# A gated recurrence's level products repacked to 128x128, with the second half of the tokens reversed

## The chip, the cores and the metric

One core of a Trainium2 chip runs the whole kernel in one launch. The metric is the device time of one execution in microseconds (us). TensorE is called PE, its weight loads PEld, VectorE DVE, ScalarE ACT, GpSimd POOL, and SyncE SP, which here only issues loads of weights and inputs.

## The reference

Two decoder layers over 256 tokens of width 1024, in float32, each followed by a SwiGLU feed-forward block (FFN). Layer 0 mixes tokens with a gated linear recurrence (8 heads, 128 key features each), layer 1 with causal attention and a relative-position bias. The change is mostly in layer 0:

```python
q = silu(q); f = lb + (1 - lb) * sigmoid(fz); k = 1 - f
S_t = diag(f_t) S_{t-1} + k_t i_t^T          # per head
o_t = S_t^T q_t
```

Written as scores this is `score[t, s] = sum_n q[t,n] k[s,n] prod(f[s+1..t, n])` for s <= t, and `o = score @ i`. The diagonal `score[t, t] = sum_n q[t,n] k[t,n]` has no decay. In layer 1, with 256 tokens in one block, attention is plain causal attention: `softmax(q k^T / sqrt(128) + bias[t - s])`.

## The kernel before

**Products.** A float32 matrix product is made of three products of the type fp32r: every operand is split into a rounded high part and a remainder (`whi`, `wlo` of a weight, `xh`, `xl` of an activation), and PE adds high x high, high x low, low x high (`mm_w`, L479, moves 256 tokens per product; `mm_x`, L488, moves 512 weight columns). These are called weight products here. Weights come from memory in pieces of 128x1024 (`raw`, issued on SP, L401); ACT rounds each (L412) and DVE takes the remainder (L414), six pieces ahead. The products of the recurrence itself are plain f32, issued by `mm` (L454).

**A head of the recurrence** (`class Core`, L724). Features lie on partitions, tokens on columns. Three projections of 24 weight products each come one after another, forget, query and gate, and their work goes on while PE makes the next ones.
- `forget` (L736): sigmoid, `f` and `k1 = 1 - f` on ACT; six products on POOL (`tot`, L752) give the decay over 2, 4, ... 64 tokens.
- `query` (L755): silu into `mov` on DVE, `q1 = q f`, and ACT puts the odd columns of `q1` behind `mov`.
- `step` (L778), for m = 1, 2, ... 32: from the queries and keys of blocks of m tokens to those of 2m: DVE scales the later half of the queries (L785) and the earlier half of the keys (L787) by the decay of the other half, ACT copies the other halves over (L789, L792). So a block's queries are scaled by the decay since its start, and its keys by the decay until its end. At m = 32 ACT makes two rearranging copies more (L799, L801), and for 64 `last` (L809) scales the queries and keys that meet across token 128.
- `scores` (L816): PE multiplies keys by queries. The scores within a pair of blocks of m tokens are one "level"; a mask picks the right entries. The diagonal and level 1 come from two products of 192 columns (128 from `mov`, 64 from `q1`), levels 2, 4, 8, 16 from two products of 64 columns each (one for either half of 128 tokens), levels 32 and 64 from two products of 128 columns (`both`, L857), and the tokens across 128 from one (L862). DVE's `copy_predicated` (L844, L827) moves each level from PSUM into the score tile `pm` under its mask; ACT moves the large blocks (`far`, L866, five copies). `values` (L880) multiplies `i` by `pm`, 256 and 128 columns. Token order is ascending, so in either half of 128 tokens the later tokens look back at the earlier ones.

**The order of the work.** `Order` (L136) simulates the engines with nominal costs while the program is built. An instruction goes to its engine's queue when the simulated clock finds its inputs ready, the lowest due time first; instructions of PE outside the weight products are put in only when their inputs have been ready for 1500 ns by those costs (`early`, `pick` L218). The queues of the engines are in that order on the chip, and each waits for its inputs on semaphores.

**Bias and final factors.** A table of the bias by distance (384 distances) is made by one product (L937) and written to memory, and eight loads issued by POOL (L941) spread it into `bt`, 128x(8x256). The final norm's gains are later loaded into the same place (`gf`, L1136, issued on ACT) and scaled on ACT (L1137).

**Names that the prediction uses.** psA and psB are the two sets of four PSUM banks. `pv` holds the norm gains, loaded by a DMA that ACT's queue issues (L517). `sqacc` and `ny` are the row statistics of a norm.

Of the kernel before, what the change touches and what calls it, by code (L numbers as in the profile page):

```python
# [8 lines left out]
FT = mybir.dt.float32  # L9
# [6 lines left out]
P = 128  # L16
# [13 lines left out]
LEVELS = (1, 2, 4, 8, 16)  # L30
# [252 lines left out]
def cv(n, fast=False):  # L283
    return ((n / 2 if fast else n) + 66) / 0.96
# [18 lines left out]
def hybrid_trunk(ctx: ExitStack, tc: tile.TileContext, wts, xT, par, gfin, tab, onehot, masks, out):  # L303
# [14 lines left out]

    def new(tag, shape, bufs=1, dt=FT, held=False):
        return ring(tag, shape, bufs, dt).new(held)  # L320
# [187 lines left out]
    make_identity(nc, ident)  # L508
    wb = main_bank("A")
# [15 lines left out]
    bt = new("bt", [P, NH * S])  # L525
# [3 lines left out]
    oh = fixed("oh", [33, 384])  # L529
    tb = fixed("tb", [33, NH])  # L530
    V.memset(tb[32:33, :], MASKED)
    od.op("S", 60, lambda: nc.sync.dma_start(oh.tile, onehot), writes=[oh], nbytes=60000, due=100)
# [190 lines left out]

    class Core:  # L724
# [3 lines left out]
        def __init__(self, h):  # L728
            self.h = h
            self.f = new("ff", [P, S], 2)  # L730
            self.so = new("so", [P, S], 3)
            self.Q = {m: new(f"q{m}", [P, S], 2) for m in (1, 2, 4, 8, 16, 32, 64)}
            self.K = {m: new(f"k{m}", [P, S], 2) for m in (1, 2, 4, 8, 16, 32, 64)}
            self.tot = {1: self.f}

        def forget(self, b):  # L736
# [6 lines left out]
            k1 = self.K[1]  # L743
# [11 lines left out]
        def query(self, b):  # L755
            f, q1 = self.f, self.Q[1]
            b, src = normed(self.h, b, 6)
            sg = new("sgq", [P, S], 3)
            self.mov = mov = new("mov", [P, 2, 192], 2)
            two = lambda t: t.rearrange("p (a t) -> p a t", a=2)  # L760
            od.op("A", ca(S), lambda: A.activation(sg.tile, src(), AF.Sigmoid), reads=[b], alloc=[sg], due=6)
            od.op("V", cv(S), lambda: V.tensor_tensor(mov[:, :, :P], two(src()), two(sg.tile), op=OP.mult),
                  reads=[b, sg], alloc=[mov], due=6)
            od.op("V", cv(S), lambda: V.tensor_tensor(two(q1.tile), mov[:, :, :P], two(f.tile), op=OP.mult),
                  reads=[mov, f], alloc=[q1], due=7)
            od.op("A", ca(P), lambda: A.activation(
                mov[:, :, P:], q1.tile.rearrange("p (a t z) -> p a t z", a=2, z=2)[:, :, :, 1], AF.Copy),
                reads=[q1], writes=[mov], due=8)
# [9 lines left out]
        def step(self, m, due):  # L778
            Q, K, tot = self.Q, self.K, self.tot[m]
            nb = S // (2 * m)  # L780
            if m < 64:
                q, qn, k, kn = Q[m], Q[2 * m], K[m], K[2 * m]
                v4 = lambda t: t.tile.rearrange("p (b z m) -> p b z m", z=2, m=m)
                bc = lambda z: tot.tile.rearrange("p (b z) -> p b z", z=2)[:, :, z:z + 1].to_broadcast([P, nb, m])
                od.op("V", cv(P), lambda: V.tensor_tensor(v4(qn)[:, :, 1], v4(q)[:, :, 1], bc(0), op=OP.mult),  # L785
                      reads=[q, tot], alloc=[qn], due=due)
                od.op("V", cv(P), lambda: V.tensor_tensor(v4(kn)[:, :, 0], v4(k)[:, :, 0], bc(1), op=OP.mult),  # L787
                      reads=[k, tot], alloc=[kn], due=due)
                o = od.op("A", ca(P), lambda: A.activation(v4(qn)[:, :, 0], v4(q)[:, :, 0], AF.Copy), reads=[q],  # L789
                          writes=[qn], due=due + .1)  # L790
                o.deps.append(qn.writers[0])
                o = od.op("A", ca(P), lambda: A.activation(v4(kn)[:, :, 1], v4(k)[:, :, 1], AF.Copy), reads=[k],  # L792
                          writes=[kn], due=due + .1)
                o.deps.append(kn.writers[0])
                if m == 32:


                    v2 = lambda t: t.tile.rearrange("p (a x) -> p a x", a=2)
                    od.op("A", ca(64), lambda: A.activation(v2(k)[:, :, 96:128], v2(kn)[:, :, 0:32], AF.Copy), reads=[kn],  # L799
                          writes=[k], due=due + .2)  # L800
                    od.op("A", ca(P), lambda: A.activation(  # L801
                        q.tile.rearrange("p (a y z x) -> p a y z x", a=2, y=2, z=2)[:, :, :, 0],
                        v2(qn)[:, :, 64:128].rearrange("p a (y x) -> p a y x", y=2), AF.Copy), reads=[qn], writes=[q],
                        due=due + .2)
                return
            self.q128, self.k128 = q, k = new("q128", [P, P], 2), new("k128", [P, P], 2)
            Q, K = Q[64], K[64]

            def last():  # L809
                A.activation(q[:, 64:], Q[:, 192:], AF.Copy, scale=tot[:, 2:3])  # L810
                A.activation(q[:, :64], Q[:, P:192], AF.Copy)
                A.activation(k[:, :64], K[:, :64], AF.Copy, scale=tot[:, 1:2])
                A.activation(k[:, 64:], K[:, 64:P], AF.Copy)
            od.op("A", 4 * ca(64) + 186, last, reads=[Q, K, tot], alloc=[q, k], due=due)

        def scores(self, due):  # L816
            h, Q, K, mov = self.h, self.Q, self.K, self.mov
# [3 lines left out]
            def take(b, c, m, stride=64):  # L821
                dst = pm.tile.rearrange("p a (b z m) -> p a b z m", z=2, m=m)
# [468 lines left out]
```

## Time and profile before

| | us |
|---|---|
| Median of three runs | 629.03 (627.8 to 629.64) |
| Span of the profiled execution | 629.2 |
| PE busy | 617.4 |
| DVE busy | 441.0 |
| ACT busy | 364.2 |
| POOL busy | 39.2 |
| Recurrence: first and last value product start | 57.8, 137.0 |

No time is listed for the profiled execution other than its span, which is 0.2 us above the median of the runs. In the profile a matmul's record lasts until its modelled end, and records overlap: the busy time of PE counts the stretch that they cover, and what a product costs the stream is read from the distance between starts. Rows of the waits name the engine that waited, the one that released it, the total, how often, and the longest. Rows of the timeline give start, duration, engine, line, operation, out<-in, partitions x columns of the stationary operand, and the moving operand.

### The profile page before, as it was taken

The numbers are of one execution on the slowest core, as the hardware profiler recorded it, in microseconds if no ns is written. First come the engines' busy times: TensorE is split into PE (matmuls) and PEld (weight loads), VectorE is DVE, ScalarE is ACT, GpSimd is POOL, SyncE is SP. The second block draws the span as 40 slices with busy tenths as digits, with TensorE's granted clock in tenths as the row PEclk, the third lists the DMA queues.
The fourth block names the chain that finished last, engine by engine and source line by source line (L and its number), as shares of the span: only waits on it lengthen the run. The fifth ranks groups of instructions, "written<-read, shape, count | busy, mean of one in ns | idle before, by whom it ended". The sixth has DMA issues, their size and how long they took to land.

```text
span 629.2 us, 12441 instructions
## 1 busy us (share of the span) xinstructions
PE 617.4 (98%) x4848; PEld 594.2 (94%) x4848; DVE 441.0 (70%) x800; ACT 364.2 (58%) x715; POOL 39.2 (6%) x74
## 2 busy tenths in 40 slices
PE   7999999999999999999999999999999999999995
PEld 5899999999999999999998899999899999999994
DVE  5898878877786666666659678866686666666653
ACT  6798888875564444444446566564674444444443
POOL 0132112200400000000000000000100000000003
PEclk9999999999999999999999999999999999999998
DMA  8964443534896666666653564445545665555501
GB/s 273 324 217 136 154 128 123 155 115 134 209 282 200 194 199 198 190 189 198 201 189 116 209 223 160 143 154 182 180 160 197 201 199 197 177 188 176 168 1 67
DMA packets 32135, 111.83 MB, mean 178 GB/s; under 512 B 3835, under 2 KB 4508, under 8 KB 32076
## 3 DMA queue, kind: packets, MB, share of 16 engines
q1 hardware_dynamic: 31052, 108.71, 53.4%
q0 software_dynamic: 448, 1.25, 1.0%
q10 hardware_dynamic: 576, 1.08, 0.6%
q8 instruction: 38, 0.62, 0.4%
q14 instruction: 21, 0.17, 0.1%
HBM read 109.78 MB, written 1.25 MB: 176 GB/s over the span
## 4 chain that ended last, share of the span: by engine, by line
PE 78%; issue 16%; DVE 3%; DMA 1%; ACT 1%; POOL 1%; SPq 0%; ACTq 0%; DVEq 0%; POOLq 0%
PE psB L455 44%; PE psA L455 33%; DMA raw<-in_w_dram 1%; DVE wlo L414 1%; POOL ny L591 1%; DVE xl L541 0%; DVE yt L607 0%; ACT whi L412 0%; DVE hT L609 0%; DVE sqacc L559 0%; PE psB L1146 0%; SPq L401 0%; SPq L522 0%; PE psA L596 0%; DVE raw L1177 0%
## 5 line engine op out<-in xcount | busy, mean ns | idle before, releaser
L414 DVE TENSOR_TENSOR wlo<-raw,whi 128x1024 fp32r<-128x1024 f32 (+1 forms) x206 | 247.8, 1213 | 107.8 <-ACT whi L412 107.4
L412 ACT ACTIVATE whi<-raw 128x1024 fp32r<-128x1024 f32 (+1 forms) x205 | 213.0, 1050 | 145.7 <-issue 66.7
L455 PE MATMUL psB<-xh,whi 128*128 128x256 f32 x608 | 172.6, 287 | 0.0
L455 PE MATMUL psB<-xh,wlo 128*128 128x256 f32 x608 | 167.6, 279 | 0.0
L455 PE MATMUL psB<-xl,whi 128*128 128x256 f32 x608 | 163.3, 279 | 0.0
L455 PE MATMUL psA<-xh,whi 128*128 128x256 f32 x544 | 150.3, 280 | 0.0
L455 PE MATMUL psA<-xh,wlo 128*128 128x256 f32 x544 | 148.8, 277 | 0.0
L455 PE MATMUL psA<-xl,whi 128*128 128x256 f32 x544 | 144.0, 277 | 0.0
L455 PEld LDWEIGHTS psB<-xh,wlo 128*128 128x128 f32 x608 | 114.6, 188 | 0.7
L455 PEld LDWEIGHTS psB<-xh,whi 128*128 128x128 f32 x608 | 114.4, 188 | 0.8
L455 PEld LDWEIGHTS psB<-xl,whi 128*128 128x128 f32 x608 | 112.2, 189 | 0.0
L455 PEld LDWEIGHTS psA<-xh,whi 128*128 128x128 f32 x544 | 102.4, 188 | 0.6 <-issue 0.5
L455 PEld LDWEIGHTS psA<-xh,wlo 128*128 128x128 f32 x544 | 102.2, 188 | 0.0
L455 PEld LDWEIGHTS psA<-xl,whi 128*128 128x128 f32 x544 | 99.2, 188 | 0.0
L455 PE MATMUL psB<-hl,whi 128*128 128x256 f32 x176 | 48.7, 277 | 0.0
L455 PE MATMUL psB<-hh,whi 128*128 128x256 f32 x176 | 48.7, 277 | 0.0
L455 PE MATMUL psB<-hh,wlo 128*128 128x256 f32 x176 | 48.7, 276 | 0.0
L957 ACT ACTIVATE u<-sgq 128x256 f32<-128x256 f32 x44 | 18.0, 410 | 38.9 <-DVE sgq L955 38.7
L455 PE MATMUL psA<-wlo,hh 128*128 128x512 f32 x88 | 34.6, 393 | 0.0
L455 PE MATMUL psA<-whi,hl 128*128 128x512 f32 x88 | 34.5, 392 | 0.0
L455 PE MATMUL psA<-whi,hh 128*128 128x512 f32 x88 | 34.5, 392 | 0.0
L455 PEld LDWEIGHTS psB<-hl,whi 128*128 128x128 f32 x176 | 33.1, 188 | 0.0
(178 smaller groups left out, 793.8 us busy)
## 6 DMA issues: line engine op xcount, KB each, us to landing
raw<-in_w_dram SPq DMA_DIRECT2D x202, 512.0 KB, 4.2
raw<-in_w_dram SPq DMA_DIRECT2D x4, 256.0 KB, 3.3
bt<-scr POOLq DMA_DIRECT2D x8, 128.0 KB, 9.1
hT<-in_x_dram SPq DMA_DIRECT2D x4, 128.0 KB, 5.1
hT<-in_x_dram SPq DMA_DIRECT2D x2, 256.0 KB, 8.1
bt<-in_final_dram ACTq DMA_DIRECT2D x1, 512.0 KB, 5.4
out_dram<-raw ACTq DMA_DIRECT2D x2, 256.0 KB, 2.2
out_dram<-raw SPq DMA_DIRECT2D x2, 256.0 KB, 2.0
```

The lines of the kernel that those rows point to most:

```text
L412: od.op("A", ca(n), lambda h=h, r=r, o=o, n=n: A.activation(h[:, :n], r[:, o:o + n], AF.Copy), reads=[r], alloc=[h], due=due)
L414: od.op("V", cv(n), lambda h=h, lo=lo, r=r, o=o, n=n: V.tensor_tensor(lo[:, :n], r[:, o:o + n], h[:, :n].bitcast(FT), op=OP.subtract), rea ...
L455: T.matmul(o, a, b, start=start, stop=stop, skip_group_check=True)
L591: od.op("G", 500, lambda: G.tensor_tensor(y.tile, v.tile, mhalf, op=OP.pow), reads=[v], alloc=[y], due=due)
L957: od.op("A", ca(S), lambda: A.activation(sg.tile, gs.tile, AF.Sigmoid), reads=[gs], alloc=[sg], due=due)
```

## The change

The level structure stays, but tokens 128 to 255 are stored in reverse (the input is reversed before the launch, the output after it). In that half the earlier token of a pair now stands at the higher column, so it is the mirror image of the first half, and access patterns with a step of P - m or P + m between the halves reach both.

- **Levels.** Queries and keys are scaled in place (one `q`, one `k` tile a head). Before that, ACT packs the 128 earlier keys and the 128 later queries of the level, of both halves, into one tile `e`: two copies for every level, 64 among them. A level is then one product of 128 packed keys by 128 packed queries; the keys' packing puts each key on the partition where its token stands, so that one masked copy takes both halves. Level 32 goes the same way (new mask), so `far` has three copies instead of five.
- **Diagonal.** POOL multiplies query by key, ACT rounds the result, POOL takes the remainder, and PE adds both over the partitions with a tile of ones: two fp32r products of 256 columns. POOL's first product reads the key tile that level 1 scales in place.
- **Bias.** The distances run both ways, so the table has 512 entries, `bt` is 128x(8x384), and POOL issues sixteen loads.
- **The ones** are made once on ACT, from the identity.
- **Final factors.** Their scaling is due at 300 instead of 100 on the planner's scale.

```diff
-LEVELS = (1, 2, 4, 8, 16)
+LEVELS = (1, 2, 4, 8, 16, 32)
...
+    def walk(t, offset, *dims):
+        a = t[:, :]
+        return bass.AP(tensor=a.tensor, offset=a.offset + offset, ap=[a.ap[0], *[list(d) for d in dims]])
+    def picked(t, m, late):
+        return walk(t, m if late else 0, [P - m if late else P + m, 2], [2 * m, 64 // m], [1, m])
...
+    allone = sb.tile([P, P], FR, name="allone")
+    A.activation(allone, ident, AF.Copy, scale=0.0, bias=1.0)
...
+            self.E = {m: new(f"q{m}", [P, S], 2) for m in (1, 2, 4, 8, 16, 32, 64)}
+            self.k, self.q, e, self.far, eh, el = (new(f"k{i}", [P, S], 2) for i in (1, 2, 4, 8, 16, 32))
+            self.own = [e, rings["eh"].new(), rings["el"].new()]
...
+            od.op("V", cv(S), lambda: V.tensor_tensor(sg.tile, src(), sg.tile, op=OP.mult), reads=[b, sg], writes=[sg],
+                  due=6)
+            od.op("V", cv(S), lambda: V.tensor_tensor(q1.tile, sg.tile, f.tile, op=OP.mult), reads=[sg, f], alloc=[q1],
+                  due=7)
+            od.op("G", cg(S), lambda: G.tensor_tensor(own[0].tile, sg.tile, k1.tile, op=OP.mult), reads=[sg, k1],
+                  alloc=[own[0]], due=8)
+            od.op("A", ca(S), lambda: A.activation(own[1].tile, own[0].tile, AF.Copy), reads=[own[0]], alloc=[own[1]], due=12)
+            od.op("G", cg(S), lambda: G.tensor_tensor(own[2].tile, own[0].tile, own[1].tile.bitcast(FT), op=OP.subtract),
+                  reads=own[:2], alloc=[own[2]], due=14)
...
+            late, early = (lambda: picked(q.tile, m, 1)), (lambda: picked(k.tile, m, 0))
+            flat = lambda c: e[:, c:c + P].rearrange("p (a b x) -> p a b x", a=2, x=m)
+            keys = lambda: e[:, :P].rearrange("p (b a x) -> p a b x", a=2, x=m)
+            od.op("A", ca(P), lambda: A.activation(keys(), early(), AF.Copy), reads=[k], alloc=[e], due=due)
+            o = od.op("A", ca(P), lambda: A.activation(flat(P), late(), AF.Copy), reads=[q], writes=[e], due=due)
...
+                by = lambda z: walk(tot.tile, z, [P // m + 1 - 2 * z, 2], [2, nb], [0, m])
+                od.op("V", cv(P), lambda: V.tensor_tensor(early(), early(), by(1), op=OP.mult),
+                      reads=[k, tot], writes=[k], due=due)
+                od.op("V", cv(P), lambda: V.tensor_tensor(late(), late(), by(0), op=OP.mult),
+                      reads=[q, tot], writes=[q], due=due)
...
             def level(b, c, m):
-                o = Q[m].tile.rearrange("p (a b z m) -> p a b z m", a=2, z=2, m=m)[:, :, :, 1]
-                for a in range(2):
-                    mm(b[:P - m, c + 64 * a:c + 64 * a + 64], K[m][:, a * P:a * P + P - m], o[:, a], start=True, stop=True)
+                mm(b[:, c:c + P], E[m][:, :P], E[m][:, P:], start=True, stop=True)
...
             def s0():
-                for a in range(2):
-                    mm(b0[:, 192 * a:192 * a + 192], K[1][:, a * P:a * P + P], mov[:, a], start=(a == 0), stop=True)
-            od.op("T", 2 * ct(192), s0, reads=[K[1], mov], alloc=[b0], due=due)
+                for i in (1, 2):
+                    mm(b0[:, :S], allone, own[i].tile, start=(i == 1), stop=(i == 2))
+            last = od.op("T", 2 * MM, s0, reads=own[1:], alloc=[b0], due=due)
...
+            for m in LEVELS:
+                if c == 4 * P or m == 16:
+                    b, c, last = bank("A"), 0, None
+                o = od.op("T", 220, lambda b=b, c=c, m=m: level(b, c, m), reads=[E[m]], due=due,
+                          **(dict(writes=[b]) if last else dict(alloc=[b])))
...
+            o2 = od.op("T", 220, lambda: level(b3, 0, 64), reads=[E[64]], alloc=[b3], due=due)
+            o3 = od.op("T", 220, lambda: mm(b3[:, P:2 * P], w[:, :P], w[:, P:], start=True, stop=True),
...
             def far():
+                A.activation(pm[0:64, 0, 64:], b3[0:64, :64], AF.Copy)
+                A.activation(pm[64:, 2, :64], b3[64:, 64:P], AF.Copy)
+                A.activation(pm[:, 1, :], b3[:, P:2 * P], AF.Copy)
...
+    od.op("T", ct(512), lambda: mm(eb[:, :], tbr.tile, oh.tile, start=True, stop=True), reads=[tbr, oh], alloc=[eb], due=80)
...
+        for c0, n, at, step in ((0, P, REP * a, 1), (P, S, S - 1 - REP * a, -1)):
+            od.op("G", 1000, lambda a=a, c0=c0, n=n, at=at, step=step: G.dma_start(
...
     od.op("A", ca(D), lambda: A.activation(gf.tile, gf.tile, AF.Copy, scale=-(float(D) ** 0.5) / 2), reads=[bt],
-          writes=[gf], due=100)
+          writes=[gf], due=300)
...
+    order = np.r_[:P, S - 1:P - 1:-1]
+    xT = np.ascontiguousarray(a["x"][0][order].T.reshape(KT, P, S).transpose(1, 0, 2))
```

**Where instructions stand.** PE, in the middle of the recurrence, where products of neighbouring heads mix (`mov,k` is the diagonal with level 1, `q,k` a level, `pm,ii` the values, `xh,whi` and the like weight products; x2 is two products). Before:

```order
L455 MATMUL psA<-q_1089,k_1045 128x128 x2
L455 MATMUL psA<-mov,k_1094 128x192 x2
L455 MATMUL psA<-q_1153,k_1126 126x64 x2
L455 MATMUL psB<-xh_404,whi 128x256
L455 MATMUL psB<-xh_404,wlo 128x256
L455 MATMUL psB<-xl_411,whi 128x256
```

After (`eh` and `el` are the diagonal's two parts, `q` alone is a packed level):

```order
L464 MATMUL psB<-xl_518,whi 128x256
L464 MATMUL psA<-q_1292 128x128
L464 MATMUL psA<-eh,allone 128x256
L464 MATMUL psA<-el,allone 128x256
L464 MATMUL psB<-xh_365,whi 128x256
L464 MATMUL psB<-xh_365,wlo 128x256
L464 MATMUL psB<-xl_374,whi 128x256
L464 MATMUL psA<-q_1339 128x128
```

Pairs of 192, 128 and 64 columns have become single products of 128 and two of 256. From the query's last weight product to the ones products of its head there are now 63, 42, 48, 48, 48, 48, 48 and 39 weight products in the eight heads. The last head's value products stand behind 783 weight products of the program, where it was 744; the output projection first reads that head's result at 816.

ACT at the program's start, before and after:

```order
L502 ACTIVATE warm<-warm 128x1
L517 DMA pv<-in_par_dram 128x64
L539 ACTIVATE xh_163<-hT,pv 128x256
L412 ACTIVATE whi<-raw 128x512
L539 ACTIVATE xh_175<-hT,pv 128x256
```

```order
L511 ACTIVATE warm<-warm 128x1
L519 ACTIVATE allone<-ident 128x128
L528 DMA pv<-in_par_dram 128x64
L550 ACTIVATE xh_165<-hT,pv 128x256
L421 ACTIVATE whi<-raw 128x512
```

The instruction for the ones, which reads the identity that POOL makes, stands in front of the issue of the gains' load.

ACT after the attention layer, where the final factors are loaded and scaled, before and after:

```order
L539 ACTIVATE xh_6025<-hT,pv 128x256
L1136 DMA bt<-in_final_dram 128x1024
L558 ACTIVATE sq<-hT 128x512
L1137 ACTIVATE bt<-bt 128x1024
L539 ACTIVATE xh_6072<-hT,pv 128x256
```

```order
L550 ACTIVATE xh_5987<-hT,pv 128x256
L1132 DMA bt<-in_final_dram 128x1024
L569 ACTIVATE sq<-hT 128x512
L1133 ACTIVATE bt<-bt 128x1024
L550 ACTIVATE xh_6034<-hT,pv 128x256
```

The later due time leaves the scaling where it stood, one square behind the issue of its load. On POOL, a head's two new products stand behind its six decay products, in two heads behind five of them; of the sixteen bias loads six stand ahead of the first FFN's row statistic (four of eight before), and the bias product stands behind 880 weight products (898 before).

More of the change, by code (lines that the diff above doesn't have):

```diff
@@ L524, in hybrid_trunk @@
     NMK = 2 * P + 64 * 2 * len(LEVELS)
-    bt = new("bt", [P, NH * S])
+    bt = new("bt", [P, NH * 3 * P])
     bt.tile = bt.ring.make()
@@ L807, in step @@
-            Q, K = Q[64], K[64]
+            w = self.far
             def last():
[L810 to L814, printed above, removed]
+                A.activation(w[:, :64], k[:, :64], AF.Copy, scale=tot[:, 1:2])
+                A.activation(w[:, 64:P], k[:, 64:P], AF.Copy)
+                A.activation(w[:, P:192], q[:, P:192], AF.Copy, scale=tot[:, 3:4])
+                A.activation(w[:, 192:], q[:, 192:], AF.Copy)
@@ L855, in scores @@
-            b3 = bank("A")
-            def both():
-                for a in range(2):
-                    c = slice(a * P, a * P + P)
-                    mm(b3[:, c], K[32][:, c], Q[32][:, c], start=True, stop=True)
-            o2 = od.op("T", 2 * ct(P), both, reads=[K[32], Q[32]], alloc=[b3], due=due)
-            o3 = od.op("T", ct(P), lambda: mm(b3[:, 2 * P:3 * P], self.k128.tile, self.q128.tile, start=True, stop=True),
-                       reads=[self.k128, self.q128], writes=[b3], due=due)
+            b, c = b0, S
@@ new lines, in scores @@
+            for m in LEVELS:
[3 more added lines that the diff above has]
+                          **(dict(writes=[b]) if last else dict(alloc=[b])))
+                if last:
+                    o.deps.append(last)
+                last = o
+                od.op("V", cv(P), lambda b=b, c=c, m=m: take(b, c, m), reads=[b, mk], writes=[pm], due=due)
+                c += P
@@ L877, in scores @@
+                A.activation(pm[64:, 2, :64], b3[64:, 64:P], AF.Copy)
+                A.activation(pm[:, 1, :], b3[:, P:2 * P], AF.Copy)
+            od.op("A", 500, far, reads=[b3], writes=[pm], due=due)
             b4 = bank("A")
@@ L928, in hybrid_trunk @@
     REP = 16
-    scr = dr.tile([P, 384], FT, name="scr")
+    scr = dr.tile([P, 512], FT, name="scr")
     scr_b = Buf(None)
-    e = new("be", [P, 384])
+    e = rings["lg"].new()
     eb = bank("B")
@@ L1133, in hybrid_trunk @@
     st3.finish("A", 40)
-    gf = new("bt", [P, NH * S])
+    gf = new("bt", None)
     gf.tile = bt.tile[:, :D]
@@ L1248, in _constants @@
     import numpy as np
-    onehot = np.zeros((33, 384), np.float32)
-    for i in range(384):
-        dist = 255 - i
+    onehot = np.zeros((33, 512), np.float32)
+    for i in range(512):
+        dist = 255 - i if i < S else i - 383
         if dist < 0:
```

120 lines of the change are left out of this document (37 added, 83 removed).

## The prediction

> **What bounds the kernel now.** I read the page's busy shares and its chain first, then what TensorE waited for, then the stage that the change rewrites.
>
> ```profile
> PE 617.4 (98%) x4848; PEld 594.2 (94%) x4848; DVE 441.0 (70%) x800; ACT 364.2 (58%) x715; POOL 39.2 (6%) x74
> ...
> PE 78%; issue 16%; DVE 3%; DMA 1%; ACT 1%; POOL 1%; SPq 0%; ACTq 0%; DVEq 0%; POOLq 0%
> ```
>
> ```profile
> PE psA L455 <- POOL ident masks.py:199: 1.4, 1, 1.4
> PE psB L455 <- ACT whi L412: 1.1, 1, 1.1
> PE psB L455 <- DVE wlo L414: 0.9, 2, 0.8
> PE psA L455 <- DVE sqacc L580: 0.8, 1, 0.8
> PE psA L596 <- POOL ny L591: 0.5, 1, 0.5
> ```
>
> These five rows (total, times, longest) are all that TensorE (PE) waited for: 4.7 us of a span of 629.2, the first three of them at the start. PE is the chain, so a product taken away shortens the kernel, unless another engine is late next. That is read in the recurrence, here six stretches of 12 us from 55 to 127 us:
>
> ```profile
> sum 72.00, PE 72.00 PEld 71.69 DVE 57.98 ACT 61.40 POOL 14.04; mean PE 12.00 PEld 11.95 DVE 9.66 ACT 10.23 POOL 2.34
> ```
>
> PE is full, DVE busy 81%, ACT 85%. So there is room on both, though not much.
>
> **TensorE in a head.** A busy time of overlapping products is no price; the distance of starts is. Below, a row is start, duration, engine, and an f32 product leaves two records (x4 is a pair).
>
> ```profile
> 122.63 0.51 PE L455 MATMUL psA<-q,k 128*112 128x64 f32 x4
> 122.95 0.36 PE L455 MATMUL psB<-xh,whi 128*128 128x256 f32 x1
> 123.15 0.28 PE L455 MATMUL psB<-xh,wlo 128*128 128x256 f32 x1
> ...
> 123.62 0.28 PE L455 MATMUL psB<-xl,whi 128*128 128x256 f32 x1
> 123.74 0.81 PE L455 MATMUL psA<-mov,k 128*128 128x192 f32 x4
> 124.26 0.42 PE L455 MATMUL psB<-xh,whi 128*128 128x256 f32 x1
> 124.51 0.28 PE L455 MATMUL psB<-xh,wlo 128*128 128x256 f32 x1
> ...
> 124.75 0.61 PE L455 MATMUL psA<-q,k 128*128 128x128 f32 x4
> 125.11 0.37 PE L455 MATMUL psB<-xh,whi 128*128 128x256 f32 x1
> 125.31 0.28 PE L455 MATMUL psB<-xh,wlo 128*128 128x256 f32 x1
> ...
> 125.89 0.55 PE L455 MATMUL psA<-q,k 128*126 128x64 f32 x4
> 126.25 0.36 PE L455 MATMUL psB<-xh,whi 128*128 128x256 f32 x1
> 126.45 0.28 PE L455 MATMUL psB<-xh,wlo 128*128 128x256 f32 x1
> ```
>
> ```profile
> 133.52 0.38 PE L455 MATMUL psA<-q,k 128*128 128x128 f32 x2
> 133.66 0.36 PE L455 MATMUL psB<-xh,whi 128*128 128x256 f32 x1
> 133.86 0.28 PE L455 MATMUL psB<-xh,wlo 128*128 128x256 f32 x1
> ```
>
> From 123.15 to 123.62 are four steps of an fp32r product of 256 columns: 0.118 us each. From the start of an f32 group to the second fp32r product behind it, less 0.118 for the first, is the group's price. The 192-column pair costs 124.51 - 123.74 - 0.118 = 0.65; the two 64-column products of level 16 cost 0.40 and of level 2 0.44, so four such levels 4 x 0.42 = 1.69; the pair at 124.75 costs 0.44; the single product of 128 columns 133.86 - 133.52 - 0.118 = 0.22. The point is that a product of 64 columns (0.20 to 0.22) is no cheaper than one of 128.
>
> Before, a head: 0.65 + 1.69 + 0.44 + 0.22 = 3.00. After: two fp32r products of 256 columns against the ones (0.24) and eight f32 products of 128 columns (six levels, 64, and the far one; 1.78), together 2.02. The shapes of the eight stand in the trace. Saved: 0.98 a head, 7.9 us in eight heads. The value products and all weight products stay.
>
> **The bias product** has 512 columns for 384:
>
> ```profile
> L455 PE MATMUL psB<-oh,tbr 33*128 33x384 f32 x2 | 0.9, 534 | 0.0
> ```
>
> A third of 0.9 more is +0.3. The bias copies on the POOL queue, sixteen for eight, end by about 172 us where they ended at 168 (0.53 us each, rows of L941 below), and the first logits that read them come at 367.7: nothing, with 195 us of cover. On POOL a row statistic of the first FFN stands behind six of them instead of four, but they start 18 weight products (2 us) earlier, so it isn't later either.
>
> **VectorE and ScalarE.**
>
> ```profile
> L827 DVE COPY_PREDICATED pm<-mk,psA 120x128 f32<-120x128 uint8 x8 | 2.3, 287 | 0.0
> L744 ACT ACTIVATE k<-ff 128x256 f32<-128x256 f32 x7 | 2.9, 408 | 0.0
> ```
>
> DVE gains one masked copy a head (level 32): +0.29. The scalings keep their 128 elements, now in place, so each waits for ACT's packing copy of its level; what queues behind on DVE is the weight split. ACT issues 22 instructions a head for 24, one of them 256 wide (0.41): unchanged. A head takes 72 fp32r products (8.5), 3.0, and value products of 384 columns (three times 0.22): 12.2 us, later 11.2. DVE's 81% of 12.2 is 9.8, with the copy 10.1: 90% of 11.2. ACT's 85% becomes 93%. Both still fit. Behind the last head its value products stand 33 weight products ahead of their first use in the output projection, where it was 72: 3.9 us of cover for one DVE, one ACT and one DVE instruction of 256 columns (0.4 to 0.5 each); nothing, and what is missing of the 3.9 if queues eat it.
>
> **POOL** gets two products of 128x256 a head. Neither stands in the trace; the rows around them do (min/median/max ns, then first and last start in us):
>
> ```profile
> L785 DVE TENSOR_TENSOR q<-q,tot x40: 270/288/383, 44.3 to 129.3; 128x128 f32<-128x128 f32 x40
> L752 POOL TENSOR_TENSOR tot<-ff x8: 400/402/1278, 38.8 to 119.6; 128x128 f32<-128x128 f32 x8
> ```
>
> ```profile
> L1080 DVE CUSTOM_DVE_ANT_0 lg<-psB,bt x16: 281/356/422, 367.7 to 414.4; 128x128 f32<-128x128 f32 x8, 128x256 f32<-128x256 f32 x8
> L941 POOL DMA_DIRECT2D bt<-scr x8: 530/532/575, 160.5 to 167.3; - x8
> L1182 POOL TENSOR_TENSOR raw<-raw,bt x4: 1291/1292/1434, 614.9 to 623.0; 128x512 f32<-128x512 f32 x4
> ```
>
> Between 0.40 at 128 columns and 1.29 at 512, a third of the way up: 0.70 each. The 1278 beside a median of 402 shows POOL products held up by 0.9 at times; so up to 1.6 each. Does it hold up DVE in turn? The page "SBUF — State Buffer" of the Trainium skill (section "Who interferes with whom") says that a VectorE instruction with two SBUF inputs and a GpSimd one that reads SBUF exclude each other for a whole instruction, whoever is first. The 1278 agrees for one direction. That rule is the first rival.
>
> A second thing hangs on POOL: its first product reads the keys, and level 1 scales them in place. So the whole chain of levels now starts behind the query's POOL product, where the keys' chain started right after the forget projection. DVE's and ACT's later instructions of that head, and weight splits queued behind them, move back with it; the order plans for that with POOL at its nominal cost.
>
> For waits of PE in the recurrence, between 0 (the planned order holds) and 2.6 (the first rival), I take 0.8, nearer to the lower end, since DVE has 10% left and ACT 7%.
>
> **Start and end.** The ones are made on ACT from the identity, ahead of the issue of the gains' load:
>
> ```profile
> 0.91 0.39 ACTq L517 DMA_DIRECT2D pv<-in_par_dram  x1
> ...
> 11.44 1.06 ACT L412 ACTIVATE whi<-raw 128x1024 fp32r<-128x1024 f32 x1 [0.79 <-DMA raw<-in_w_dram]
> ```
>
> ```profile
> 12.55 0.50 PE L455 MATMUL psB<-whi,xh 128*128 128x512 f32 x1 [1.05 <-ACT whi L412]
> ...
> 15.37 0.63 PE L455 MATMUL psB<-whi,xh 128*128 128x512 f32 x1
> ```
>
> PE had the identity 1.4 us into its wait (first row above), and so will ACT; the gains are issued at 1.4 for 0.91, land 0.5 us later, and so do the first products. The cover is the 1.05 that PE waits at 12.55 for weights whose load nothing here delays: nothing at the end; without cover 0.5. Behind it 512-column products run at half pace (0.63 each) for some 2.6 us, worth up to 1.3; with the gap shortened they may go, or not.
>
> The final factors have a later due time, but the order has their scaling at the same place on ACT, between the same square and split:
>
> ```profile
> 438.66 1.06 ACT L1137 ACTIVATE bt<-bt 128x1024 f32<-128x1024 f32 x1 [2.78 <-DMA bt<-in_final_dram]
> ```
>
> Its wait of 2.78 stays, and the 0.8 and 0.5 of PE behind it. That this part doesn't do what it says costs and brings nothing; were it moved, 1.3 would go.
>
> **Pace.** The chain of waits shows one thing that the sum cannot hold: 48 equal products take
>
> ```profile
> 192.31 5.44 PE psA L455 x48
> ...
> 585.89 5.66 PE psB L455 x48
> ```
>
> in two places, with nothing waited for. Each FFN has 18 such blocks, so a whole FFN at the other pace is 4 us. I know no reason for the pace, and a changed stream may move it: -2 (the second FFN's slow half turns quick) to +4 (the first one slow).
>
> **Sum.** 629.2 - 7.9 + 0.3 + 0.8 = 622.4 for the profiled execution's span. The only other measure of that execution is the median of three runs, 629.03 (627.8 to 629.64), 0.2 below; so 622.2.
>
> **Rivals.**
> 1. VectorE becomes the bound. If each of the two POOL products holds up a two-input DVE product for its whole 0.70, DVE needs 10.1 + 1.4 = 11.5 a head against a PE pitch of 11.2. Eight heads give back 2.6: 629.2 - 7.6 + 2.6 = 624.2, and up to 626.5 with uneven queues. For it: 90% on DVE without this. Against: DVE's scalings beside POOL's six products a head have a median (288) near their minimum (270), and at most 0.1 more. The Trainium skill's rule above would give this case. 0.18.
> 2. Slower: the diagonal comes too late. It now runs sigmoid (ACT, 0.41), product (DVE, about the same), product (POOL, 0.70), rounding (ACT, 0.41), subtraction (POOL, 0.70): 2.6 us, before PE may issue the ones products, and level 1 waits for the first three of these steps too. These stand 39 to 63, mostly 48, weight products behind the query's last: 48 x 0.118 = 5.7. If both POOL steps are held up (+0.9 each), two of the six decay products ahead of them too (+1.8), and a weight copy stands in front on ACT (+1.0), the chain is 7.2 and PE, whose queue is in order, waits 1.5 a head: 629.2 - 7.6 + 12 = 633.6. It decides from 0.95 a head on. Against: it needs nearly every hold-up in nearly every head. 0.07.
> 3. No change: the recurrence saves 7.9 but the pace turns slow in the first FFN (+4) and DVE binds (+2.6): 628.5. 0.05.
> 4. More than forecast: no waits, the half-speed stretch gone, quick pace to the end: 629.2 - 7.6 - 1.3 - 2 = 618.3. 0.04.
>
> The forecast itself (620 to 624) has 0.66. The range takes in rival 1 and most of the pace: 619.2 to 627.0. About 0.3% (1.9 us) is what a measurement of this kernel can tell from no change. Faster by more than that: forecast, rivals 1 and 4, 0.88; within, rival 3, 0.05; slower, rival 2, 0.07.
>
> **What would show it.** Right: PE full in the recurrence; the last value product about 8 us earlier in the span; the eight products of a head 0.22 each; POOL's new products near 0.70; the FFN blocks at 5.44 to 5.66. Rival 1: waits of PE on DVE or ACT (weights, packed tiles) in that stretch, DVE over 95% busy. Rival 2: PE waiting for POOL in front of the ones products. The prediction is wrong if the recurrence is shorter by less than 5 us, or if the ones products or eight products cost over 2.3 a head.

## The result, and the profile after

The changed kernel is slower: 633.66 us median (633.15 to 635.83) against 629.31 (627.8 to 629.64), a ratio of 1.0071 with a 95% interval of 1.0057 to 1.0085. The forecast was 622.2. The profiled execution took 633.8 us with a span of 632.0. In all runs with both numbers the time is about 1.8 to 2.2 above the span; so the profiled execution of before (span 629.2) was one of about 631.0, 1.7 above its median. That is why the spans differ by 2.8 and the medians by 4.35.

The page after, busy shares and chain:

```profile
PE 612.3 (97%) x4784; PEld 587.6 (93%) x4784; DVE 446.5 (71%) x808; ACT 362.3 (57%) x700; POOL 58.1 (9%) x98
...
PE 68%; issue 17%; DVE 7%; ACT 4%; POOL 2%; DMA 2%; SPq 0%; DVEq 0%; ACTq 0%; POOLq 0%
```

PE does 5.1 us less and the span is longer. What PE waited for in the changed kernel (total, times, longest):

```profile
PE psB L464 <- ACT xh L550: 8.1, 1, 8.1
PE psA L464 <- POOL ident masks.py:199: 1.4, 1, 1.4
PE psA L464 <- DVE sqacc L591: 1.2, 1, 1.2
PE psA L464 <- DVE pm L829: 0.6, 2, 0.3
PE psA L607 <- POOL ny L602: 0.4, 1, 0.4
PE psA L464 <- ACT pm L866: 0.3, 1, 0.3
PE psA L464 <- DVE pm L844: 0.3, 1, 0.3
PE psA L464 <- ACT q L803: 0.2, 1, 0.2
```

One wait of 8.1 stands ahead of the first weight product. The chain of waits of the changed kernel shows where it comes from (start, duration, what):

```profile
1.65 3.14 DMA raw<-in_w_dram
4.79 0.02 issue
4.81 6.86 DMA pv<-in_par_dram
...
11.76 0.51 ACT xh L550
...
13.26 0.76 PE psB L464
```

The gains' load was issued at 4.81, where it was 0.91, and took 6.86 to land, where it took 2.5. And 4.79 is the moment at which a weight load of SP's, the third load of the program, had landed.

The recurrence, the same six stretches of 12 us as before:

```profile
sum 72.00, PE 70.77 PEld 68.55 DVE 65.35 ACT 62.43 POOL 28.07; mean PE 11.80 PEld 11.42 DVE 10.89 ACT 10.41 POOL 4.68
```

PE has holes now (70.77 of 72, where it was full), DVE is busy 91% instead of 81%, POOL twice as long. The products themselves cost what was forecast:

```profile
96.13 0.38 PE L464 MATMUL psA<-q 128*128 128x128 f32 x2
96.27 0.36 PE L464 MATMUL psA<-eh,allone 128*128 128x256 f32 x1
96.47 0.28 PE L464 MATMUL psA<-el,allone 128*128 128x256 f32 x1
96.58 0.28 PE L464 MATMUL psB<-xh,whi 128*128 128x256 f32 x1
96.70 0.28 PE L464 MATMUL psB<-xh,wlo 128*128 128x256 f32 x1
...
98.56 0.39 PE L464 MATMUL psA<-q 128*128 128x128 f32 x2
98.70 0.37 PE L464 MATMUL psB<-xh,whi 128*128 128x256 f32 x1
98.91 0.28 PE L464 MATMUL psB<-xh,wlo 128*128 128x256 f32 x1
```

A single product costs 98.91 - 98.56 - 0.118 = 0.23; the group with the two ones products 96.70 - 96.13 - 0.118 = 0.45, so these two cost 0.22. A head has 8 x 0.23 + 0.22 = 2.06.

To see where time is won or lost, the 4440 weight products of the kernels can be numbered and the start of the n-th compared: number 96 is the first of the recurrence's projections, 863 the last of the output projection, behind the last value product. The differences to the profiled execution of before, in us (one execution of each kernel: that of a1 was 1.1 below the median of its runs, so a microsecond in the last column says little):

| kernel | at 96 | at 863 | recurrence | at 900 | last |
|---|---|---|---|---|---|
| after | +6.2 | +2.8 | -3.4 | +2.9 | +2.8 |
| b1_before_ones_early | +5.3 | +5.3 | 0.0 | +5.3 | +5.2 |
| a1_ones_behind_load | -1.4 | -4.8 | -3.4 | -4.8 | -5.3 |
| a4_remainder_on_vector | -0.9 | -7.3 | -6.4 | -7.2 | -7.4 |
| a5_diagonal_on_vector | -1.1 | -7.9 | -6.9 | -4.1 | -4.5 |
| a7_gpsimd_twice | -0.8 | -1.1 | -0.3 | -1.1 | -0.9 |
| a8_vector_once_more | -0.9 | -2.5 | -1.6 | -2.5 | -3.2 |

So two things went wrong, and they can be told apart: the start lost 6 to 7 us, and the recurrence gave back 3.4 where the prices of its products give 8 x (3.00 - 2.06) = 7.5. The other 4.1 are waits. The rows above list 1.4 of them; most of the rest is hidden where the records overlap, but the starts show it: a single level between two weight products costs 0.14 at best and 0.67 at worst, and all groups of products together cost 4.1 more than the shortest group of the same kind in any kernel with the change. After that nothing happens: +2.8 at product 863 and +2.8 at the last.

### The profile page after: what moved, and what is told of

The parts are those of the page before. It is cut to its first block, busy times and chain, and to the rows that moved or that the text cites. A ratio compares the mean times of both kernels' runs of the same rounds, so it can differ in the third digit from the quotient of the medians.

```text
span 632.0 us, 12218 instructions
## 1 busy us (share of the span) xinstructions
PE 612.3 (97%) x4784; PEld 587.6 (93%) x4784; DVE 446.5 (71%) x808; ACT 362.3 (57%) x700; POOL 58.1 (9%) x98
## 4 chain that ended last, share of the span: by engine, by line
PE 68%; issue 17%; DVE 7%; ACT 4%; POOL 2%; DMA 2%; SPq 0%; DVEq 0%; ACTq 0%; POOLq 0%
PE psB L464 37%; PE psA L464 31%; DVE wlo L423 2%; ACT whi L421 1%; POOL tot L767 1%; DMA pv<-in_par_dram 1%; DVE pm L829 1%; DVE k L809 1%; DVE k L807 1%; POOL ny L602 1%; DMA raw<-in_w_dram 0%; DVE xl L552 0%; DVE xl L888 0%; DVE yt L618 0%; ACT q L802 0%
## 5 line engine op out<-in xcount | busy, mean ns | idle before, releaser
L423 DVE TENSOR_TENSOR wlo<-raw,whi 128x1024 fp32r<-128x1024 f32 (+1 forms) x206 | 249.5, 1221 | 101.7 <-ACT whi L421 101.5
L602 POOL TENSOR_TENSOR ny<-nv,mhalf 128x2 f32<-128x2 f32 x5 | 6.4, 1286 | 318.6 <-DVE nv L599 318.6
```

What stands on the lines that cost most here:

```text
L423: od.op("V", cv(n), lambda h=h, lo=lo, r=r, o=o, n=n: V.tensor_tensor(lo[:, :n], r[:, o:o + n], h[:, :n].bitcast(FT), op=OP.subtract), rea ...
L602: od.op("G", 500, lambda: G.tensor_tensor(y.tile, v.tile, mhalf, op=OP.pow), reads=[v], alloc=[y], due=due)
```

## The experiments

Their times were taken beside the kernel before on the same chip (630.27, 629.94, 629.92 and 630.55 us in the four series); the ratio compares best.

### The start

**b1: the kernel before, with the ones instruction alone.**

```diff
+    allone = sb.tile([P, P], FR, name="allone")
+    A.activation(allone, ident, AF.Copy, scale=0.0, bias=1.0)
     wb = main_bank("A")
```

> The kernel before, with one thing added: the ones tile (unused here) is made by ScalarE from the identity ahead of the issue of the gains' load, as the change has it. Theory S (the start: the late gains cost the change about 6 us): the load is issued near 4.8 us for 0.91 and lands near 11.7, the first weight product starts near 13.3 us for 4.96, and the time is 5 to 7 us above the kernel before, 634.5 to 636.5. The prediction's step (lands 0.5 us later and is covered): no more than 0.5 us above, 629.3 to 629.8.

637.03 us, ratio 1.0115 (1.0096 to 1.0134): 7.2 us (6.0 to 8.4) lost by one instruction of 0.29 us whose result is not used; 5.2 between the two profiled executions. That is Theory S, and a little above its 5 to 7. The issue of the load in its timeline:

```profile
4.75 0.39 ACTq L519 DMA_DIRECT2D pv<-in_par_dram  x1
...
13.21 0.77 PE L455 MATMUL psB<-whi,xh 128*128 128x512 f32 x1 [8.07 <-ACT xh L541]
```

**a1: the changed kernel, the ones behind the load.** Nothing else moves in the order.

```diff
-    A.activation(allone, ident, AF.Copy, scale=0.0, bias=1.0)
...
-    od.op("S", 60, lambda: A.dma_start(pv.tile, par), ...)
+    def load_gains():
+        A.dma_start(pv.tile, par)
+        A.activation(allone, ident, AF.Copy, scale=0.0, bias=1.0)
+    od.op("S", 60, load_gains, ...)
```

> The changed kernel with one move: the ones tile is made right behind the issue of the gains' load instead of ahead of it; every other instruction stays in its place. Theory S with a weak recurrence (the start costs 6.2 us, the recurrence gives back only 3.5): 633.7 - 6.2 = 627.5, that is 1.8 us below the kernel before. Rival R1 (the waits in the recurrence came from the late start too, so the forecast holds once the start is mended): 622 to 624. Rival R2 (the recurrence waits for its chain of levels however early it starts, so the gain at the start is lost again): 630 to 633.

626.81 us, 0.9949 (0.9935 to 0.9963). The start is worth 1.0071 - 0.9949 = 1.2%, 7.7 us, and the recurrence still gives 3.4, so the weak recurrence is a second matter: R1, which had it mended with the start, and R2, which had the start's gain lost again, both fall.

```profile
0.91 0.39 ACTq L528 DMA_DIRECT2D pv<-in_par_dram  x1
2.14 0.29 ACT L529 ACTIVATE allone<-ident 128x128 fp32r<-128x128 f32 x1
```

That a1 is 1.4 ahead of the kernel before at product 96, though both start their first weight product at 5.0, is another matter. From 15 to 18 us, before and in a1 (the third number from the end is the granted clock of PE, 1.00 in full):

```profile
15.00:18.00 3.00, 3.00 (x9) 2.33 (x8) 3.00 (x6) 3.00 (x7) 0.00 (x0) 0.50 1.00 341
```

```profile
15.00:18.00 3.00, 2.89 (x13) 2.05 (x11) 3.00 (x7) 2.57 (x4) 0.00 (x0) 1.00 1.03 410
```

The kernel before makes these products at half the clock, a1 doesn't; the changed kernel has 0.50 there too.

**a2 and p1: the ones first, the load issued by another engine.** In a2 `A.dma_start(pv.tile, par)` becomes `nc.sync.dma_start`, in p1 `G.dma_start`.

> The changed kernel, ones first on ScalarE as it has them, but the gains' load is issued by SyncE ahead of its own loads instead of by ScalarE. Theory S (the loss at the start is the place of that load behind the others, not the ones instruction itself): the load lands near 3.3 us and the time is that of the kernel with the ones behind the load, 626.5 to 627.5 (the first input is issued 0.4 us later). If the ones instruction itself or what it does to ScalarE cost the time: 631 to 634.

> The changed kernel, ones first on ScalarE, and the gains' load issued by GpSimd right behind the identity, at about 1.4 us, when SyncE has issued three loads. Theory Q (a load that is asked for once SyncE issues load on load gets its turn only behind them): issued near 4.8 us or landing near 11, 632 to 634. Rival (only the time at which its engine comes to it counts): issued at 1.4, landing at about 4, first weight product at 5.5, 627 to 628.5.

a2: 627.80 us, 0.9958 (0.9939 to 0.9976). p1: 626.79 us, 0.9944 (0.9927 to 0.9962). Both are near a1, so the ones instruction costs nothing that these runs can tell (a2 is 0.3 above its range), and Theory Q in the form in which p1 tested it (a load asked for once SP's issues run gets its turn behind them) finds no support: POOL got its issue at 1.45, between SP's at 1.19 and 1.66. In p1's trace this load reports to a semaphore that no load of SP or ACT uses, so p1 doesn't test the semaphores of those two engines.

```profile
1.45 0.76 POOL L528 DMA_DIRECT2D pv<-in_par_dram  x1
5.02 0.51 ACT L550 ACTIVATE xh<-hT,pv 128x256 fp32r<-128x256 f32 x1 [2.58 <-DMA pv<-in_par_dram]
```

**s1: the ones first on ACT, but without a wait for POOL.** What holds ACT's issue from 2.43 (ones done) to 4.81 stands in the program, in the waits of its instructions. ACT in the changed kernel, and in the kernel before:

```
3 L519 ACTIVATE allone<-ident 128x128 [waits Pool_49]
4 L528 DMA pv<-in_par_dram 128x64 [waits DMAHW2_49]

3 L517 DMA pv<-in_par_dram 128x64
4 L539 ACTIVATE xh_163<-hT,pv 128x256 [waits DMAHW3_49,DMAHW0_49]
```

A completion semaphore is a counter that tells when a load has landed. In this program the loads of SP and ACT are given eight of them in turn. Before, the gains' load is the fourth and gets number 3. Behind an instruction that waits for POOL it is placed later, comes behind ten of SP's, and gets number 2 a second time: it is not issued before the first user of number 2, SP's third load, has landed, at 4.79. The traces agree: the issue waits for the semaphore that the load issued at 1.65 reports to, in the changed kernel and in b1, and for none in the kernel before, a1 and s1.

```diff
-    A.activation(allone, ident, AF.Copy, scale=0.0, bias=1.0)
+    A.activation(allone, warm.to_broadcast([P, P]), AF.Copy, scale=0.0, bias=1.0)
```

> The changed kernel with the ones still made by ScalarE ahead of the issue of the gains' load, but from the one-column tile that ScalarE itself has just written, instead of from GpSimd's identity: the same instruction, without a wait for another engine. In the program of the change the gains' load comes after eight loads of SyncE in the order in which loads are given one of eight completion semaphores, so its issue waits until the third of them has landed; in this kernel it comes second and waits for none. Theory Q (that wait is what makes the start late): issued at 0.9 to 2.5 us, landing by 5, first weight product at 5 to 6, and 626.5 to 627.5. Rival (an instruction of ScalarE ahead of the issue is enough to put it behind SyncE's loads): issued near 4.8 us, 632 to 634.

628.75 us, 0.9965 (0.9949 to 0.9982): between the two, and above the range of Theory Q, which has the issue right (2.27) and the landing wrong (used from 6.90, not by 5). (The load is the fourth again, not the second as the expectation has it, and in the change it stands behind ten loads, not eight.)

```profile
2.27 0.31 ACT L519 ACTIVATE allone<-warm 128x128 fp32r<-128x128 f32 x1
2.27 0.38 ACTq L528 DMA_DIRECT2D pv<-in_par_dram  x1
...
6.97 0.51 ACT L550 ACTIVATE xh<-hT,pv 128x256 fp32r<-128x256 f32 x1 [4.39 <-DMA pv<-in_par_dram]
```

The semaphore's wait is gone, and the issue comes at 2.27: the ones read what ACT's own first activation writes, which ends behind ACT's table load, and the issue stands behind them. At product 96 the five kernels stand at -1.4 (issued at 0.91), -0.7 (0.74, by SP), -1.2 (1.45, by POOL), +1.1 (2.27) and +6.2 (4.81). Of the change's 7.6 against a1, 2.5 are the later place on ACT, and 5.1 the used semaphore; in both parts is a longer landing, 4.6 and 6.9 for 2.5.

### The recurrence

**a3: level 1 freed from POOL.** ACT makes a second copy of the keys for POOL's product.

```diff
+            k2 = self.k2 = new("k64", [P, S], 2)
+            od.op("A", ca(S), lambda: A.activation(k2.tile, f.tile, AF.Identity, scale=-1.0, bias=1.0), reads=[f], ...)
...
-            k1 = self.k
+            k1 = self.k2
```

> The changed kernel with the ones behind the load, and a second copy of the keys made by ScalarE for GpSimd's diagonal product, so that level 1 may scale the keys in place without waiting for GpSimd; one more ScalarE instruction of 256 columns a head (0.41 us). Theory L (TensorE waits in the recurrence because the levels start behind GpSimd's product): 2 to 3 us below the kernel with the ones behind the load alone, near 625. Rival D (it waits because VectorE is nearly full, its instructions lengthened by GpSimd's): within 1 us of that kernel, or up to 1.5 us above it by the added ScalarE work.

630.69 us, 1.0014 (0.9997 to 1.0031). In the recurrence it wins 3.2 like a1 (3.4), so Theory L finds no support, though the copy adds 0.41 a head to ACT and may hide a small gain. The 4 us by which it is slower than a1 are lost between products 863 and 900, ahead of the first FFN (see a5).

**a4: the diagonal's subtraction on DVE.**

```diff
-            od.op("G", cg(S), lambda: G.tensor_tensor(own[2].tile, ..., op=OP.subtract),
+            od.op("V", cv(S), lambda: V.tensor_tensor(own[2].tile, ..., op=OP.subtract),
```

> The changed kernel with the ones behind the load, and the subtraction of the diagonal (the remainder of the split) on VectorE instead of GpSimd: VectorE gets 0.42 us a head more, GpSimd's 1.03 us a head go. Rival D (GpSimd's instructions lengthen VectorE's, by more than 0.42 a head): no slower than the kernel with the ones behind the load, 0 to 2 us below it. Theory L (the late start of the levels is what matters, and VectorE only has 10% left): 0 to 2.5 us above it.

624.19 us, 0.9911 (0.9896 to 0.9926). DVE has more to do, and the kernel gains 2.6 us on a1, more than the 2 that Rival D expected: the recurrence gives 6.4. This is the fastest version, below both kernels. The order that the planner makes is another one here, so this run alone doesn't say that POOL is the cause; a7 does, in which the order stays. Its stretches of the recurrence:

```profile
sum 72.00, PE 71.63 PEld 70.97 DVE 67.82 ACT 64.44 POOL 17.50; mean PE 11.94 PEld 11.83 DVE 11.30 ACT 10.74 POOL 2.92
```

DVE at 94% and PE nearly full: the share of DVE alone is not what makes PE wait.

**a7 and a8: one more instruction, the order unchanged.** a7 has POOL's subtraction twice, a8 DVE's product of queries and decays twice, the second into a tile that is not read.

```diff
+                G.tensor_tensor(spare.tile, own[0].tile, own[1].tile.bitcast(FT), op=OP.subtract)
```

```diff
+                V.tensor_tensor(spare.tile, sg.tile, f.tile, op=OP.mult)
```

> The kernel with the ones behind the load, and GpSimd's subtraction of the diagonal issued twice in each head: the second goes into a spare tile that nobody reads. The order of all other instructions is the same. Theory D (GpSimd's two-input instructions lengthen VectorE's, and VectorE has no room): another 1.0 us of it a head costs 2 to 5 us, 629 to 632 beside 626.8. Theory L (only who waits for GpSimd matters): within 0.7 us of 626.8, since nobody waits for the spare tile.

> The kernel with the ones behind the load, and VectorE's product of the queries with the decays issued twice in each head: the second goes into a spare tile that nobody reads; the order is the same. It adds 0.42 us of VectorE a head, as much as moving the subtraction to VectorE does, while GpSimd keeps its own. Theory D (VectorE is the bound with 0.9 of its time used and stretched): 1 to 3.4 us above 626.8. If VectorE still had room: within 0.7 us.

a7: 629.95 us, 1.0000 (0.9990 to 1.0009), 3.2 us above a1 by the ratios, with nobody waiting for the second result. a8: 628.21 us, 0.9975 (0.9963 to 0.9986), 1.6 above a1. An instruction more on POOL takes twice as much from PE as one more on DVE. It might do so by delaying what stands behind it on POOL, but the waits for POOL's results in the recurrence are the same in a7 as in a1 (DVE 1.4 and 1.4, ACT 2.9 and 2.9, PE 0.2 and 0.2). What differs is DVE: its 236 instructions between products 96 and 863 are the same in both and take 118.5 us in a1, 121.7 in a7. These 3.2 us are what PE loses there (3.1). In a8 DVE gets 3.7 us more and PE loses 1.8; why only half of it counts isn't shown.

**What POOL does to DVE.** The rounding remainder of a head's result is the same instruction in all kernels; of before, after and a4 (min/median/max ns in the first two, mean in the third):

```profile
L896 DVE TENSOR_TENSOR xl<-u,xh x8: 418/422/427, 60.7 to 140.5; 128x256 fp32r<-128x256 f32 x8
```

```profile
L888 DVE TENSOR_TENSOR xl<-u,xh x8: 413/420/964, 71.5 to 146.5; 128x256 fp32r<-128x256 f32 x8
```

```profile
L891 DVE TENSOR_TENSOR xl<-u,xh 128x256 fp32r<-128x256 f32 x8 | 3.4, 423 | 0.0
```

Two of the eight took 0.96 in the changed kernel, both beside POOL's subtraction, here one:

```profile
93.94 0.96 DVE L888 TENSOR_TENSOR xl<-u,xh 128x256 fp32r<-128x256 f32 x1
```

```profile
93.51 1.11 POOL L784 TENSOR_TENSOR el<-k,eh 128x256 fp32r<-128x256 f32 x1 [1.37 <-ACT eh L783]
```

DVE's instruction starts inside POOL's and ends 0.28 behind its end. POOL's are stretched as well, to 1.03 and 0.82 where the shortest subtraction took 0.74, and in the groups of the changed kernel DVE's weight splits are longer by 4% (1221 ns before) and the keys' scalings by 13% (286 before):

```profile
L423 DVE TENSOR_TENSOR wlo<-raw,whi 128x1024 fp32r<-128x1024 f32 x34 | 43.1, 1269 | 5.6 <-ACT whi L421 5.6
L807 DVE TENSOR_TENSOR k<-k,tot 128x128 f32<-128x128 f32 x40 | 12.9, 323 | 0.9 <-ACT q L802 0.9
L784 POOL TENSOR_TENSOR el<-k,eh 128x256 fp32r<-128x256 f32 x8 | 8.3, 1032 | 9.7 <-ACT eh L783 9.7
L781 POOL TENSOR_TENSOR k<-sgq,k 128x256 f32<-128x256 f32 x8 | 6.6, 822 | 2.0 <-DVE sgq L777 1.2 <-PE psB L464 0.8
```

The Trainium skill's page "SBUF — State Buffer" (section "Who interferes with whom") says that a VectorE instruction with two SBUF inputs contends with a GpSimd instruction that reads SBUF, for an exclusive lock, and that the order of issue decides which of the two is blocked. The trace agrees, in both directions: above DVE is held up, and the subtraction that starts at 105.84, inside a weight split of DVE's (105.66 to 106.88), takes 1.64 for 0.74.

**a5: both diagonal instructions on DVE.** The diff is that of a4, and the same for `own[0]`.

> The kernel with the ones behind the load, and both diagonal instructions (the product with the keys and the subtraction) on VectorE; GpSimd has only its six decay products, as before the change. VectorE gets 0.84 us a head more than with both on GpSimd. Theory D with GpSimd's product costing VectorE more than the 0.42 it takes there: 621 to 624, below the 624.2 of the kernel with the subtraction alone moved. If VectorE is simply full: 625 to 627.

627.09 us, 0.9964 (0.9948 to 0.9979): slower than a4, far outside the expectation for Theory D and just above the other. But the recurrence gives 6.9, more than in any run with POOL at work on the diagonal. The loss is elsewhere: 3.8 us between products 863 and 900. PE at the start of the first FFN in a5:

```profile
145.92 0.39 PE L464 MATMUL psA<-xh,whi 128*128 128x256 f32 x1 [1.83 <-DVE hT L623]
...
148.21 0.28 PE L464 MATMUL psA<-xh,whi 128*128 128x256 f32 x1
148.33 0.32 PE L464 MATMUL psA<-xh,wlo 128*128 128x256 f32 x1
148.45 0.41 PE L464 MATMUL psA<-xh,whi 128*128 128x256 f32 x1
148.66 0.42 PE L464 MATMUL psA<-xh,wlo 128*128 128x256 f32 x1
148.87 0.42 PE L464 MATMUL psA<-xh,whi 128*128 128x256 f32 x1
```

A wait of 1.83 for the residual's addition, and from 148.45 on products 0.21 apart instead of 0.12, sixteen of them up to 151.86: 1.5 us more. That is the clock again:

```profile
148.40:151.90 3.50, 3.50 (x19) 3.50 (x19) 3.50 (x7) 2.68 (x6) 0.95 (x2) 0.51 0.20 75
```

On DVE the order that the simulated clock makes from a5 has two scalings of 512 columns there, then the two additions; a1 and a4 have scaling, addition, scaling. That alone isn't the cause: the kernel before has the order of a5 without this wait. What a3, a5 and a6, which lose 3.8 here, have in common is that the first scaling starts 0.25 us before product 863, where it starts 2.9 to 3.0 before it in the kernels without the loss. Why DVE comes to it that late stays open.

**c1: a5 with each residual's scaling and addition side by side.**

```diff
+            def scale_add():
+                V.tensor_tensor(t.tile, flat(), row.tile..., op=OP.mult)
+                V.tensor_tensor(h2, t.tile, h2, op=OP.add)
+            od.op("V", 2 * cv(512), scale_add, reads=[b, row], alloc=[t], writes=hb[2 * i:2 * i + 2], due=due)
```

> The kernel with both diagonal instructions on VectorE, and each residual's scaling and addition issued next to each other, so that the first hidden state is ready one VectorE instruction (0.68 us) earlier at the start of the first FFN. The kernel without this lost 3.8 us there (a wait of TensorE of 1.8 for that addition and products at half their pace behind it), after a recurrence that had given back 7.9. Theory W (that wait and the pace behind it are one event, which the order on VectorE makes): the wait falls to about 1.2, and 0.7 to 3.8 us come back: 623.3 to 626.4. Rival (the half pace comes from something else in that place): 626.4 to 627.

626.38 us, 0.9947 (0.9926 to 0.9967). In c1's trace the wait is 1.36 and the next products are 0.11 apart:

```profile
145.20 0.39 PE L464 MATMUL psA<-xh,whi 128*128 128x256 f32 x1 [1.36 <-ACT xh L553]
145.43 0.28 PE L464 MATMUL psA<-xh,wlo 128*128 128x256 f32 x1
145.54 0.28 PE L464 MATMUL psA<-xh,whi 128*128 128x256 f32 x1
```

There 1.7 are lost instead of 3.8, as Theory W has it; but the profiled execution loses 1.3 ahead of the attention layer and 2.2 ahead of the second FFN, where PE waits 1.9 for a sum of squares and the clock is 0.51 for the next 3.4 us. So the time hardly moves.

**a6: the diagonal without a split**, one f32 product with the ones; ACT's rounding and POOL's subtraction go.

```diff
-                for i in (1, 2):
-                    mm(b0[:, :S], allone, own[i].tile, start=(i == 1), stop=(i == 2))
+                mm(b0[:, :S], allone, own[0].tile, start=True, stop=True)
```

> The kernel with the ones behind the load, and the diagonal summed by one f32 product of 256 columns with the ones, without a split: ScalarE's rounding (0.41 us a head) and GpSimd's subtraction (1.03) go; TensorE pays about 0.44 for 0.25 a head, 1.5 us in all. Theory D: the 3.5 us of the subtraction come back less 1.5, 624 to 625.5; with ScalarE's relief up to 1 us less. If GpSimd's subtraction doesn't matter: 628 to 628.5.

631.12 us, 1.0010 (0.9992 to 1.0028): a miss. The recurrence gives 4.0, 0.6 more than a1; less than the 2 expected. The rest is lost outside it: 3.8 ahead of the first FFN as in a5, and 1.7 behind that, most of it ahead of the second. So this run doesn't tell much about POOL.

## Why the prediction was wrong, step by step

- **PE's products: right.** 2.06 a head for 2.02, 0.94 saved a head for 0.98, 7.5 in all for 7.9.
- **The start: the step that failed worst.** "The gains are issued at 1.4 for 0.91, land 0.5 us later" was wrong: issued at 4.81 and landed 8.3 later. Already the 1.4 was misread: that is when PE gets the identity, but ACT loads its table from 0.74 to 2.02 and comes to the ones at 2.14, and s1, without the used semaphore, has its issue at 2.27. The cover that the prediction named is real: p1's first product came 1.6 later than before, and 0.25 of it was left against a1 at product 96; s1's 3.5 became 2.5. But it covers 1.0 to 1.3 us in these two. The half-speed stretch behind it, which the prediction left open at up to 1.3, is gone in a1 and stays in the change. The prediction took the new place of a load on ACT as the only effect; the place among all loads decided which semaphore it got, and that could be seen in the program's waits without a run. b1 shows that the ones ahead of the issue alone cost 7.2 us (6.0 to 8.4).
- **Waits of PE in the recurrence: mis-sized.** 0.8 was taken, 7.5 - 3.4 = 4.1 came. The reason given, "DVE has 10% left", was the wrong measure: a4 and a5 fill DVE more and wait less. The mechanism was the one behind the prediction's first rival (POOL's products hold up DVE's), which it priced at 2.6 and judged unlikely by the median of the 128-column scalings. That median says nothing: for the queries' scalings it is 0.288 before and 0.286 after, while the longest went from 0.38 to 0.83. The rival's sign, DVE over 95% busy, didn't come (91%): PE waits though DVE isn't full. a7 and a4 put its price at about 3 us for one subtraction a head: a second costs 3.2, and with the first moved (and the order changed) the recurrence gives 3.0 more. How much of what is left is POOL's other product isn't separated; a5, without it, gives 0.5 more.
- **POOL's products**: 0.82 and 1.03 for 0.70, within the 1.6 named.
- **The level chain behind POOL** (rival 2's second half): no effect to be seen, by a3.
- **Bias product and final factors: right but for a size.** The 512-column product takes 0.64 a record for 0.53, but products 863 to 900, between which it stands in both kernels, take only 0.07 more, not 0.3. The factors' scaling still waits 2.7 for its load:

```profile
L464 PE MATMUL psB<-oh,tbr 33*128 33x512 f32 x2 | 1.1, 641 | 0.0
```

```profile
L1133 ACT ACTIVATE bt<-bt 128x1024 f32<-128x1024 f32 x1 | 1.1, 1062 | 2.7 <-DMA bt<-in_final_dram 2.7
```

- **Pace of the FFNs**: unchanged in sum, +2.9 at product 900 and +2.8 at the last.
- **Rival 2 had the time almost to the microsecond (633.6) by luck**: ahead of the ones products no row has PE waiting for POOL in the changed kernel; only its weight load did, once, for 0.2.
- **Two sums of the rivals** don't come out of their own terms: 8 x (11.5 - 11.2) is 2.4 for the 2.6 of rival 1, and 629.2 - 7.9 + 0.3 + 4 + 2.6 is 628.2 for the 628.5 of rival 3. Nothing hangs on either.

Together: the span was to fall by 6.8 and rose by 2.8. Of these 9.6, the start is 6.2 and the recurrence 3.7 (3.4 for 7.9 - 0.8 = 7.1), and the smaller bias product takes 0.2 off. The recurrence also shows the prediction's own sign of being wrong, less than 5 us gained.

With the ones behind the load and the subtraction on DVE, a4 comes near the forecast: 0.9911 (0.9896 to 0.9926), where 622.2 / 629.03 is 0.989. In part that is luck: of the 7.4 us in a4's trace 0.9 are won at the start, where the forecast had nothing, and the recurrence gives 6.4 for 7.1.

## What to carry to other kernels

When an instruction that waits is put ahead of the issue of a load, look up which completion semaphore that load gets and who used it before, not only how much later its engine comes to it. Work moved to GpSimd beside a well-filled VectorE is not free though nobody waits for its result: price it by how long VectorE's two-input instructions become, wide ones above all. Where a simulated clock sets the order, an edit in one stage can move a wait in another; compare the kernels product by product, and read the granted clock, before putting a difference down to the edit.

## What of the hardware was not expected

- The landing of one and the same 32 KB load by the time of its issue: issued at 0.74 it was used from 2.62 on, at 0.91 from 3.42, at 1.45 (by POOL) from 5.02, at 2.27 from 6.90, at 4.81 from 11.69. So many of SP's loads had been issued before it: 0, 1, 2, 4 and 9. A delay of 1.4 us in the issue (0.91 to 2.27) becomes 3.5 in the landing, and 3.9 become 8.3. That the loads ahead are what lengthens it was not tested by itself.
- After one wait of 1.83 us PE's products ran 0.21 instead of 0.12 apart for 3.4 us, some 2.5 us behind the wait, with a granted clock of 0.51; after one of 1.36 in the same place no product did. The length of the wait alone doesn't decide it: ahead of the second FFN PE waited 1.46 in s1 and 1.50 in a2, and the clock fell (0.51 for 3.4 us) in s1 only. What else decides it stays open.
